# Forgetting attention with the values stationary and the weights of a group of query tiles moving

## The chip, the core and the metric

One core of a Trainium2 chip runs the whole program in one launch. The metric is the device time of an execution in microseconds. Five engines work side by side, each through its own list of instructions in order: PE (TensorE, matmuls; PEld is its weight load), VectorE (DVE), ScalarE (ACT), GpSimd (POOL) and SyncE (SP, which issues the DMAs). They wait for each other at semaphores. A matmul keeps one operand in the array (stationary, up to 128 x 128) and streams the other through it (moving); its result goes to one of eight PSUM banks of 128 x 512 fp32.

## What is computed

Two network blocks on 1024 tokens of width 1024. The part that the change touches is one of the three mixers of the second block: a causal attention of eight heads of 64 columns, on 1040 tokens (16 learned ones ahead of the 1024), in which each score gets the difference of two running sums of logarithmic forget gates.

```python
def forgetting_attention_group(q, k, v, f_logit, f_bias):
    ...
    qh = heads(q) * (HEAD_DIM ** -0.5)
    kh = heads(k)
    vh = heads(v)
    log_f = jax.nn.log_sigmoid((f_logit + f_bias).astype(jnp.float32))
    ...
    c = jnp.cumsum(log_f, axis=1).transpose(0, 2, 1)
    ...
        s = jnp.einsum('bhqd,bhkd->bhqk', qb, kh).astype(jnp.float32) + (cb[..., :, None] - c[..., None, :])
        s = jnp.where(kpos[None, :] <= qpos[:, None], s, -jnp.inf)
        p = jax.nn.softmax(s, axis=-1)
        return jnp.einsum('bhqk,bhkd->bhqd', p.astype(vh.dtype), vh)
```

Beside it stand a gated linear recurrence (RG-LRU) and RWKV7 with a state per head; the three results are joined and go through an output projection and a feed-forward network.

## The kernel before

**Numbers.** Most matmuls take operands of the type fp32r, and a value is kept as a rounded part (hi) and the remainder (lo): `split` casts hi on ScalarE (L103) and subtracts it from the source on VectorE (L106). A product is then two or three matmuls. The last product of this attention, weights times values, is an exception: it takes plain fp32, and the trace shows two passes on PE for each such matmul.

**Tiles.** The 1040 tokens are nine query tiles: one of 16 rows and eight of 128. A head is a pair index `pr` and a half `m` (64 of 128 columns). For each head the raw queries and keys come in by DMA (tag `fraw`), and ScalarE, VectorE and GpSimd make of them `fqh`, `fql`, `fkh`, `fkc` (L1471 to L1477), each in three buffers. The values `fv` of two heads come together.

**One query tile** (`fox_tile`, L1496 to L1534). The scores of tile i against all keys up to its own end are made in pieces of 400 and up to 512 columns: two matmuls (L1506, L1507), and on the last piece a third that adds the causal mask (L1509). VectorE moves each piece from PSUM to the tile `fE` and takes the row maximum in the same pass (L397); it reduces the maxima (L1514) and changes their sign (L1515, L1517). ScalarE takes the exponential in place and the row sum (L1519), VectorE the reciprocal (L1521). Then the weights have to be turned, since a matmul sums over partitions: `wT` transposes four key tiles at a time into a bank `te` (L405) and ScalarE copies it to `wT` (L407). L1531 multiplies: the turned weights are stationary, the 64 columns of the values move, and the sum over key tiles builds up in a bank `po`. VectorE scales the 64 result columns by the reciprocal (L1532). After the second head of a pair the rows go out (L1534).

**Order.** `fox_tile` has one `yield`, between the exponential and the transposes, and `pipe` runs the items so that the scores of a tile are recorded ahead of the second half of the tile before it. In which order each engine's list is written is decided by a scheduler of the framework, which models the time of the instructions as they are recorded. RWKV's chunks (`rwkv_chunks`) are recorded before this attention, and the scheduler mixes the two; at the end of the heads `done` loads the weights of the output projection (`woraw`, `wo`, L693 with L103 and L106), and the projection follows.

**Banks.** `psum` names for each use the groups of banks that it takes in turn: groups A, B and D have two banks each, C and E one. Before this attention the line `self.psum(sc="B", te="D", po="C")` gives scores two banks, transposes two, results one; RWKV uses A and E (`ra`, `rs`).

Of the kernel before, what the change touches and what calls it, by code (L numbers as in the profile page):

```python
# [13 lines left out]
F32 = mybir.dt.float32  # L14
F32R = mybir.dt.float32r
# [16 lines left out]
class Builder:  # L32
# [1409 lines left out]
    def fox_att(self, p, qkd, vd, cnd, o2d, done):  # L1442
# [7 lines left out]
        kcs = [p.tile([128, T], F32R, name=f"fkc{i}", bufs=1) for i in range(3)]  # L1450
# [5 lines left out]
        def heads():  # L1456
            for h in range(8):
# [9 lines left out]
                qh = p.tile([128, T], F32R, tag="fqh", name="fqh", bufs=3)  # L1467
                ql = p.tile([128, T], F32R, tag="fql", name="fql", bufs=3)
                kh = p.tile([128, T], F32R, tag="fkh", name="fkh", bufs=3)
                kc = kcs[h % 3]  # L1470
# [7 lines left out]
                if m == 0:  # L1478
                    v = p.tile([128, 9, 128], F32, tag="fv", name="fv")
# [3 lines left out]
                for i in range(9):  # L1483
                    yield self.fox_tile(pr, m, i, qh, ql, kh, kc, v, o, o2d)
# [4 lines left out]
    def fox_tile(self, pr, m, i, qh, ql, kh, kc, v, o, o2d):  # L1489

        nc, p = self.nc, self.ap_
        T = 1040
        r = slice(64 * m, 64 * m + 64)
        c0, n = self.TILES[i]
        nk = c0 + n
        if i == 0:  # L1496
            cks = [(0, 16)]
        else:
            cks = [(0, min(nk, 400))] + [(a, min(512, nk - a)) for a in range(400, nk, 512)]
        E = p.tile([128, T], F32, tag="fE", name="fE", bufs=4)  # L1500
        mx = self.small(4, "fmx")
        for ci, (k0, kn) in enumerate(cks):
            sp = self.sc()
            ks = slice(k0, k0 + kn)
            last = ci == len(cks) - 1
            nc.tensor.matmul(sp[:n, :kn], qh[:, c0:c0 + n], kh[:, ks], start=True, stop=False)  # L1506
            nc.tensor.matmul(sp[:n, :kn], ql[:, c0:c0 + n], kc[:, ks], start=False, stop=not last)  # L1507
            if last:
                nc.tensor.matmul(sp[:n, kn - n:kn], self.ident_r[:n, :n], self.masks_r[:n, 2, :n],  # L1509
                                 start=False, stop=True)  # L1510
            self.evac_max(E[:n, ks], sp[:n, :kn], mx[:n, ci:ci + 1])
        nM = self.small(1, "fnM")
        if len(cks) > 1:
            nc.vector.tensor_reduce(nM[:n], mx[:n, :len(cks)], axis=AX.X, op=ALU.max)  # L1514
            nc.vector.tensor_scalar(nM[:n], nM[:n], -1.0, None, op0=ALU.mult)  # L1515
        else:
            nc.vector.tensor_scalar(nM[:n], mx[:n, :1], -1.0, None, op0=ALU.mult)  # L1517
        l = self.small(1, "fl")
        nc.scalar.activation(E[:n, :nk], E[:n, :nk], AF.Exp, bias=nM[:n], accum_out=l[:n])  # L1519
        rl = self.small(1, "frl")  # L1520
        nc.vector.reciprocal(rl[:n], l[:n])  # L1521
        yield
        ops = self.po()
        steps = [(self.wT([E[:n, 0:16]], n), 0, 0)]
        for x0 in range(1, i + 1, 4):
            grp = range(x0, min(x0 + 4, i + 1))
            w = self.wT([E[:n, self.TILES[x][0]:self.TILES[x][0] + 128] for x in grp], n)
            steps += [(w, y, x) for y, x in enumerate(grp)]
        for w, y, x in steps:
            kn = self.TILES[x][1]  # L1530
            nc.tensor.matmul(ops[:n, :64], w[:kn, y, :n], v[:kn, x, r], start=x == 0, stop=x == i)  # L1531
        nc.vector.tensor_scalar(o[:n, i, r], ops[:n, :64], rl[:n], None, op0=ALU.mult)  # L1532
        if m == 1:
            nc.sync.dma_start(o2d[i][:, pr * 128:pr * 128 + 128], o[:n, i])  # L1534
# [413 lines left out]
```

## Time and profile before

| | us |
|---|---|
| median of three runs | 3181.07 (3169.08 to 3182.06) |
| profiled execution | 3179.39 |
| its span | 3177.6 |
| PE busy in the span | 3058.7 (96%) |
| VectorE | 1863.2 (59%) |
| ScalarE | 1401.9 (44%) |
| GpSimd | 467.1 (15%) |
| this attention, from the first score matmul to the projection | 283.1 |

The span is the time from the first to the last instruction in the profile; 1.8 us of the execution lie around it. Busy time counts an engine's instructions, not its waits. The granted clock (PEclk) is the share of full TensorE speed that the chip allowed in a stretch.

### The profile page before, as it was taken

What the parts mean: (1) busy time and instruction counts of PE and PEld (TensorE: products, weight loads), DVE (VectorE), ACT (ScalarE), POOL (GpSimd) and SP (SyncE); (2) the same over time, 40 slices, a digit from 0 to 9 for tenths busy, and PEclk for the clock granted to TensorE, in tenths of its full rate; (3) what the DMA queues carried; (4) which work ended last, traced back from release to release, by engine and by line L of the source; (5) the groups of instructions that cost most, each with busy time, mean ns of one, the idle gap of its engine ahead of it and who ended that gap; (6) DMA issues with size and microseconds to landing.
All of it is one profiled execution on the core that took longest, in us unless ns stands there. A gap on an engine that the chain in (4) does not pass through costs nothing.

```text
span 3177.6 us, 52057 instructions
## 1 busy us (share of the span) xinstructions
PE 3058.7 (96%) x19891; PEld 2780.7 (88%) x19891; DVE 1863.2 (59%) x4889; ACT 1401.9 (44%) x3415; POOL 467.1 (15%) x506
## 2 busy tenths in 40 slices
PE   8899999999999999998999999999999999999997
PEld 5799999889878789997889999788879999999996
DVE  5777757677766665446547434666555344454446
ACT  4679845555553643323236121445534433233323
POOL 2467622331220000000000000201000000000003
PEclk9999999999999999999999899898999999999999
DMA  5222210110043221113321121313132111111113
GB/s 212 71 74 89 85 40 6 32 33 7 15 138 107 100 101 57 57 39 101 126 67 49 58 69 46 90 41 97 34 123 94 49 40 47 47 47 57 44 41 116
DMA packets 140330, 218.22 MB, mean 69 GB/s; under 512 B 24408, under 2 KB 80784, under 8 KB 140080
## 3 DMA queue, kind: packets, MB, share of 16 engines
q1 hardware_dynamic: 140080, 214.90, 21.5%
q8 instruction: 156, 2.56, 0.3%
q14 instruction: 94, 0.77, 0.1%
HBM read 171.87 MB, written 42.97 MB: 68 GB/s over the span
## 4 chain that ended last, share of the span: by engine, by line
PE 80%; DVE 7%; ACT 5%; DMA 3%; issue 2%; POOL 1%; SPq 0%; DVEq 0%; POOLq 0%; ACTq 0%
PE mm L132 17%; PE mm L133 16%; PE mm L134 16%; PE po L1531 3%; PE te L405 3%; PE sc L134 2%; PE sc L132 2%; PE sc L133 2%; PE sc L391 2%; PE po L661 2%; PE po L611 1%; DMA woraw<-in_w_out 1%; ACT EB L646 1%; ACT EA L596 1%; PE mm L149 1%
## 5 line engine op out<-in xcount | busy, mean ns | idle before, releaser
L132 PE MATMUL mm<-whi,hT 128*128 128x256 f32 (+1 forms) x1760 | 513.4, 292 | 15.3 <-DVE gs L428 3.4
L133 PE MATMUL mm<-wlo,hT 128*128 128x256 f32 (+1 forms) x1760 | 508.3, 289 | 3.9 <-POOL wlo L106 3.8
L132 PEld LDWEIGHTS mm<-whi,hT 128*128 128x128 f32 x1760 | 337.6, 192 | 24.1 <-ACT v L549 4.6
L133 PEld LDWEIGHTS mm<-wlo,hT 128*128 128x128 f32 x1760 | 337.7, 192 | 8.0 <-POOL wlo L106 5.1
L132 PE MATMUL mm<-hT3h,whi 128*128 128x342 f32 (+3 forms) x1020 | 325.9, 320 | 0.0
L133 PE MATMUL mm<-hT3l,whi 128*128 128x342 f32 (+3 forms) x1020 | 325.2, 319 | 0.0
L134 PE MATMUL mm<-hT3h,wlo 128*128 128x342 f32 (+3 forms) x1020 | 324.7, 318 | 0.0
L134 PE MATMUL mm<-whi,lo 128*128 128x256 f32 x1040 | 300.0, 289 | 2.5 <-POOL lo L106 2.4
L103 ACT CAST whi<-wraw 128x512 fp32r<-128x512 f32 (+2 forms) x205 | 136.0, 678 | 211.2 <-PE mm L133 85.0
L132 PE MATMUL mm<-hT,whi 128*128 128x352 f32 (+3 forms) x640 | 219.8, 344 | 2.9 <-ACT a L1018 1.8
L1659 DVE TENSOR_TENSOR acc<-acc,sc 128x512 f32<-128x512 f32 x160 | 108.8, 686 | 193.6 <-PE sc L134 192.8
L407 ACT COPY wT<-te 128x512 f32<-128x512 f32 (+2 forms) x368 | 160.5, 454 | 136.3 <-PE te L405 133.5
L133 PE MATMUL mm<-hT,whi 128*128 128x352 f32 (+3 forms) x640 | 218.7, 342 | 0.1
L134 PE MATMUL mm<-hT,wlo 128*128 128x352 f32 (+3 forms) x640 | 218.5, 343 | 0.0
L106 DVE TENSOR_TENSOR wlo<-wraw,whi 128x512 fp32r<-128x512 f32 (+1 forms) x161 | 126.0, 790 | 152.2 <-ACT whi L103 151.5
L134 PE MATMUL mm<-whi,hT 128*128 128x256 f32 (+3 forms) x720 | 205.8, 286 | 0.0
L134 PEld LDWEIGHTS mm<-whi,lo 128*128 128x128 f32 x1040 | 201.0, 193 | 5.2 <-POOL lo L106 3.3
L133 PEld LDWEIGHTS mm<-hT3l,whi 128*128 128x128 f32 x1020 | 192.0, 188 | 6.3
L132 PEld LDWEIGHTS mm<-hT3h,whi 128*128 128x128 f32 x1020 | 191.8, 188 | 6.0
L134 PEld LDWEIGHTS mm<-hT3h,wlo 128*128 128x128 f32 x1020 | 191.9, 188 | 3.6
L97 POOL TENSOR_TENSOR inv<-inv,cm 128x1 f32<-128x1 f32 (+1 forms) x87 | 53.2, 611 | 889.1 <-DVE inv L95 889.1
L97 POOL TENSOR_TENSOR c<-c,cm 128x2 f32<-128x2 f32 (+1 forms) x170 | 124.4, 733 | 384.5 <-DVE c L95 346.0
(491 smaller groups left out, 7740.8 us busy)
## 6 DMA issues: line engine op xcount, KB each, us to landing
adraw<-in_adaln_w SPq DMA_DIRECT2D x48, 512.0 KB, 3.8
wraw<-in_ffn_up SPq DMA_DIRECT2D x85, 256.0 KB, 2.8
wraw<-in_w_ab SPq DMA_DIRECT2D x26, 512.0 KB, 3.9
woraw<-in_w_out SPq DMA_DIRECT2D x48, 256.0 KB, 3.0
wraw<-in_w_gla SPq DMA_DIRECT2D x48, 256.0 KB, 2.8
wraw<-in_w_in SPq DMA_DIRECT2D x24, 512.0 KB, 4.3
dnraw<-in_ffn_down SPq DMA_DIRECT2D x44, 256.0 KB, 2.6
fraw<-qkd SPq DMA_DIRECT2D x32, 260.0 KB, 4.1
```

The costliest lines, as they stand in the source:

```text
L97: nc.gpsimd.tensor_tensor(out, out, self.cm05[:p, :n], op=ALU.pow)
L103: nc.scalar.copy(hi, src)
L106: (lo_eng or nc.vector).tensor_tensor(lo, src, hi.bitcast(F32), op=ALU.subtract)
L132: mmul(ps, ah, bh, start=k == 0, stop=False)
L133: mmul(ps, ah, bl, start=False, stop=False)
L134: mmul(ps, al, bh, start=False, stop=k == nk - 1)
L391: self.nc.tensor.matmul(sp, q[x][:, m], keys, start=x == 0, stop=last and x == 1)
L405: nc.tensor.transpose(ps[:n, j * 128:j * 128 + nq], E, self.ident[:nq, :nq])
L407: nc.scalar.copy(w[:n, :m, :nq], ps.rearrange("p (j t) -> p j t", j=4)[:n, :m, :nq])
L661: nc.tensor.matmul(ops[:, :128], w[:, x, :], v[:, i], start=x0 + x == 0, stop=x0 + x == len(kt) - 1)
L1531: nc.tensor.matmul(ops[:n, :64], w[:kn, y, :n], v[:kn, x, r], start=x == 0, stop=x == i)
L1659: nc.vector.tensor_tensor(acc[:, t, sl], acc[:, t, sl], ps, op=ALU.add)
```

## The change

One item of work is now a group of query tiles instead of one: tiles 0 to 3, 4 to 6, 7 and 8. The values become the stationary operand: `fvs` holds for each key tile the 64 columns of hi and the 64 of lo side by side, 128 columns, made once per head by ScalarE and GpSimd. For each key tile the weights of all query tiles of the group that see it are transposed into one `te` bank, side by side, up to 400 columns. `split` makes hi (`feh`, ScalarE) and lo (`fel`, VectorE, from the bank), and both move through the values in two matmuls. The result in the `po` bank has the values' columns on the partitions, so at the group's end it is copied out (`fot`), transposed back, the two halves are added and scaled. The scores are stored with their sign changed, and the minimum takes the place of the maximum. Some buffers go from three or four to two, `fv` to one, and from head 5 on the transposes have four banks and the results two.

```diff
-        kcs = [p.tile([128, T], F32R, name=f"fkc{i}", bufs=1) for i in range(3)]
+        kcs = [p.tile([128, T], F32R, name=f"fkc{i}", bufs=1) for i in range(2)]
...
-                qh = p.tile([128, T], F32R, tag="fqh", name="fqh", bufs=3)
-                ql = p.tile([128, T], F32R, tag="fql", name="fql", bufs=3)
-                kh = p.tile([128, T], F32R, tag="fkh", name="fkh", bufs=3)
-                kc = kcs[h % 3]
+                qh = p.tile([128, T], F32R, tag="fqh", name="fqh")
+                ql = p.tile([128, T], F32R, tag="fql", name="fql")
+                kh = p.tile([128, T], F32R, tag="fkh", name="fkh")
+                kc = kcs[h % 2]
...
-                for i in range(9):
-                    yield self.fox_tile(pr, m, i, qh, ql, kh, kc, v, o, o2d)
+                vs = p.tile([128, 9, 2, 64], F32R, tag="fvs", name="fvs")
+                for z in ((slice(0, 128), slice(1, 9)), (slice(0, 16), slice(0, 1))):
+                    nc.scalar.copy(vs[z][:, :, 0], v[z][:, :, r])
+                    nc.gpsimd.tensor_tensor(vs[z][:, :, 1], v[z][:, :, r], vs[z][:, :, 0].bitcast(F32), op=ALU.subtract)
+                if h == 5:
+
+                    self.psum(te="DDA", po="CE")
+                for tiles in ((0, 1, 2, 3), (4, 5, 6), (7, 8)):
+                    yield self.fox_tiles(pr, m, tiles, qh, ql, kh, kc, vs, o, o2d)
...
-            self.evac_max(E[:n, ks], sp[:n, :kn], mx[:n, ci:ci + 1])
...
-            nc.vector.tensor_scalar(nM[:n], nM[:n], -1.0, None, op0=ALU.mult)
...
+                nc.vector.tensor_scalar(E[:n, ks], sp[:n, :kn], -1.0, None, op0=ALU.mult, op1=ALU.min,
+                                        accum_out=mx[:n, ci:ci + 1])
+            if len(cks) > 1:
+                nc.vector.tensor_reduce(nM[:n, y:y + 1], mx[:n, :len(cks)], axis=AX.X, op=ALU.min)
+            nc.scalar.activation(E[:n], E[:n], AF.Exp, bias=nM[:n, y:y + 1], scale=-1.0, accum_out=l[:n, y:y + 1])
...
-        steps = [(self.wT([E[:n, 0:16]], n), 0, 0)]
-        for x0 in range(1, i + 1, 4):
-            grp = range(x0, min(x0 + 4, i + 1))
-            w = self.wT([E[:n, self.TILES[x][0]:self.TILES[x][0] + 128] for x in grp], n)
-            steps += [(w, y, x) for y, x in enumerate(grp)]
-        for w, y, x in steps:
-            kn = self.TILES[x][1]
-            nc.tensor.matmul(ops[:n, :64], w[:kn, y, :n], v[:kn, x, r], start=x == 0, stop=x == i)
-        nc.vector.tensor_scalar(o[:n, i, r], ops[:n, :64], rl[:n], None, op0=ALU.mult)
+        for x in range(tiles[-1] + 1):
+            ys = [y for y, i in enumerate(tiles) if i >= x]
+            k0, kn = self.TILES[x]
+            ps = self.te()
+            for y in ys:
+                n = cols[y].stop - cols[y].start
+                nc.tensor.transpose(ps[:kn, cols[y]], Es[y][:n, k0:k0 + kn], self.ident[:n, :n])
+            z = slice(0, kn), slice(cols[ys[0]].start, c)
+            hi = p.tile([128, 400], F32R, tag="feh", name="feh", bufs=4)
+            lo = p.tile([128, 400], F32R, tag="fel", name="fel", bufs=4)
+            self.split(hi[z], lo[z], ps[z])
+            w = vs[:kn, x].rearrange("p e d -> p (e d)")
+            for e, h in enumerate((hi, lo)):
+                nc.tensor.matmul(ops[:, z[1]], w, h[z], start=x + e == 0, stop=e == 1 and x == tiles[-1],
+                                 skip_group_check=True)
+        ot = p.tile([128, 400], F32, tag="fot", name="fot")
+        nc.scalar.copy(ot[:, :c], ops[:, :c])
+        ps = self.te().rearrange("p (y e d) -> p y e d", y=4, e=2)
+        for y in range(len(tiles)):
+            n = cols[y].stop - cols[y].start
+            nc.tensor.transpose(ps[:n, y].rearrange("p e d -> p (e d)"), ot[:, cols[y]], self.ident)
+        t = p.tile([128, 4, 64], F32, tag="ft", name="ft")
+        parts = [(slice(0, 128), slice(small, len(tiles)))] + [(slice(0, 16), slice(0, 1))] * small
+        for rows, ys in parts:
+            nc.scalar.copy(t[rows, ys], ps[rows, ys, 1])
+            nc.vector.tensor_tensor(t[rows, ys], t[rows, ys], ps[rows, ys, 0], op=ALU.add)
+            shape = [rows.stop, ys.stop - ys.start, 64]
+            nc.vector.tensor_tensor(o[rows, tiles[0] + ys.start:tiles[0] + ys.stop, r], t[rows, ys],
+                                    rl[rows, ys].unsqueeze(2).to_broadcast(shape), op=ALU.mult)
```

In the changed program the score matmuls stand in L1519, L1520 and L1522, their evacuation in L1524, the exponential in L1528, the transposes in L1543, the two new matmuls in L1550, the copy out in L1553, the transposes back in L1557, the addition in L1562 and the scaling in L1564.

The order on PE in a head before, at the passage from one query tile to the next: `po` is the result's bank, `te` the transposes', `sc` the scores'; `x5` is five in a row.

```order
L1531 MATMUL po<-fv,wT 128x64 x4
L405 MATMUL te<-ident_r,fE 16x128
L1531 MATMUL po<-fv,wT 128x64 x2
L405 MATMUL te<-ident_r,fE 128x128 x7
L1531 MATMUL po<-fv,wT 128x64 x5
L405 MATMUL te<-ident_r,fE 16x128
L1506 MATMUL sc<-fkh,fqh 128x400
L1507 MATMUL sc<-fkc_23839,fql 128x400
L1531 MATMUL po<-fv,wT 128x64 x3
L405 MATMUL te<-ident_r,fE 128x128 x8
L1531 MATMUL po<-fv,wT 128x64 x5
```

In the changed program, in a head with two transpose banks, in the group of tiles 4 to 6 (three query tiles, 384 columns):

```order
L1543 MATMUL te<-ident_r,fE 16x128 x3
L1550 MATMUL po<-feh,fvs 128x384
L1550 MATMUL po<-fel,fvs 128x384
L1543 MATMUL te<-ident_r,fE 128x128 x6
L1550 MATMUL po<-feh,fvs 128x384
L1550 MATMUL po<-fel,fvs 128x384
L1543 MATMUL te<-ident_r,fE 128x128 x2
L1550 MATMUL po<-feh,fvs 128x384
L1543 MATMUL te<-ident_r,fE 128x128
L1550 MATMUL po<-fel,fvs 128x384
L1543 MATMUL te<-ident_r,fE 128x128 x3
```

Transposes and multiplications were taken by query tile, in runs of up to eight and five; now they alternate by key tile, three transposes and the two matmuls that read what the other engines made of the bank before.

On VectorE in a head before, score evacuations (L397) with one short scaling (L1532) and one reciprocal for each query tile:

```order
L1521 RECIPROCAL frl<-fl 128x1
L397 TENSOR_SCALAR fE,fmx<-sc 128x400
L1517 TENSOR_SCALAR fnM<-fmx 128x1
L397 TENSOR_SCALAR fE,fmx<-sc 128x400
L397 TENSOR_SCALAR fE,fmx<-sc 128x128
L1514 TENSOR_REDUCE fnM<-fmx 128x1
L1515 TENSOR_SCALAR fnM<-fnM 128x1
L1532 TENSOR_SCALAR fo<-po,frl 128x64
L1521 RECIPROCAL frl<-fl 128x1
L397 TENSOR_SCALAR fE,fmx<-sc 128x400
```

In the changed program the remainders (`fel` from the bank `te` and `feh`) stand between the score evacuations (L1524):

```order
L106 TENSOR_TENSOR fel<-te,feh 128x256
L1564 TENSOR_TENSOR fo<-ft,frl 128x3x64
L106 TENSOR_TENSOR fel<-te,feh 128x256 x6
L1524 TENSOR_SCALAR fE,fmx<-sc 128x400
L1524 TENSOR_SCALAR fE,fmx<-sc 128x128
L106 TENSOR_TENSOR fel<-te,feh 128x128
L1527 TENSOR_REDUCE fnM<-fmx 128x1
L1524 TENSOR_SCALAR fE,fmx<-sc 128x400
L106 TENSOR_TENSOR fel<-te,feh 16x400
L1524 TENSOR_SCALAR fE,fmx<-sc 128x256
L1524 TENSOR_SCALAR fE,fmx<-sc 128x400
L1527 TENSOR_REDUCE fnM<-fmx 128x1
```

The short scalings per query tile are gone, and L106 takes their place in larger number: each of these passes reads a whole bank's columns.

## Rows read from the trace of the kernel before

**Rows 1.** Windows of the attention: times, engines' busy us, granted clock, DMA share, GB/s

```profile
2022.60:2180.30 157.70, 157.42 (x1136) 137.39 (x1137) 113.29 (x413) 75.97 (x188) 22.36 (x23) 0.96 0.21 51
2180.30:2214.10 33.80, 31.93 (x172) 27.51 (x170) 20.02 (x73) 19.80 (x50) 2.79 (x2) 0.70 0.57 159
2214.10:2247.20 33.10, 30.27 (x193) 24.91 (x190) 21.91 (x78) 21.45 (x54) 2.96 (x2) 0.85 0.22 69
2247.20:2269.10 21.90, 21.86 (x166) 19.31 (x165) 11.70 (x58) 13.09 (x38) 0.00 (x0) 1.00 0.06 16
2269.10:2305.70 36.60, 36.17 (x278) 31.95 (x278) 14.81 (x73) 20.00 (x54) 0.00 (x0) 1.00 0.10 26
sum 283.10, PE 277.65 PEld 241.06 DVE 181.74 ACT 150.32 POOL 28.11; mean PE 55.53 PEld 48.21 DVE 36.35 ACT 30.06 POOL 5.62
```

**Rows 2.** Chain of waits from 2247 to 2270 us: start, duration, instructions

```profile
by line: PE po L1531 52.0%; PE te L405 21.5%; PE sc L1506 12.8%; PE sc L1507 10.2%; PE sc L1509 3.7%; issue 0.2%
...
2246.99 0.45 PE po L1531 x4
...
2256.61 0.88 PE te L405 x8
2257.49 1.40 PE po L1531 x10
...
2269.43 0.64 PE po L1531 x4
```

**Rows 3.** Timeline 484 to 487 us, in the first block: start, duration, instruction

```profile
484.01 0.38 PE L379 MATMUL tp<-ident_r,qn 128*128 128x128 f32 x2
...
484.62 0.37 ACT L103 CAST qTh<-tp 128x256 fp32r<-128x256 f32 x1
...
485.02 0.42 DVE L106 TENSOR_TENSOR qTl<-tp,qTh 128x256 fp32r<-128x256 f32 x1
...
485.22 0.28 PE L133 MATMUL mm<-wlo,hT 128*128 128x256 f32 x1
...
485.34 0.28 PE L134 MATMUL mm<-whi,lo 128*128 128x256 f32 x1
```

**Rows 4.** Timeline from 2208.9 us

```profile
2209.02 0.34 PE L1507 MATMUL sc<-fkc,fql 128*128 128x400 f32 x1
...
2209.20 0.40 PE L1506 MATMUL sc<-fkh,fqh 128*128 128x512 f32 x1
```

**Rows 5.** Groups of VectorE, shapes apart, 2022.6 to 2305.7 us: busy, mean ns | idle

```profile
L1532 DVE TENSOR_SCALAR fo<-po,frl 128x64 f32<-128x64 f32 x64 | 18.0, 281 | 38.3 <-PE po L1531 37.8
L1477 DVE TENSOR_TENSOR fkh<-fraw,fkh 64x1040 fp32r<-64x1040 f32 x7 | 10.6, 1509 | 1.8 <-ACT fkh L1475 1.6
...
L1521 DVE RECIPROCAL frl<-fl 128x1 f32<-128x1 f32 x64 | 10.2, 160 | 4.5 <-ACT fE L1519 1.9
...
L1472 DVE SCALAR_TENSOR_TENSOR fql<-fraw,fqh 64x1040 fp32r<-64x1040 f32 x7 | 9.1, 1301 | 1.6 <-DMA bd<-B 1.1 <-ACT fqh L1471 0.5
L1515 DVE TENSOR_SCALAR fnM<-fnM 128x1 f32<-128x1 f32 x40 | 5.8, 145 | 0.4
...
L1256 DVE TENSOR_TENSOR S<-STP,rs 64x128 f32<-64x128 f32 x8 | 2.3, 284 | 3.2 <-PE rs L1252 3.1
```

**Rows 6.** Groups of VectorE, shapes apart, whole span

```profile
L106 DVE TENSOR_TENSOR wo<-te,wo 128x512 fp32r<-128x512 f32 x26 | 17.8, 683 | 0.6 <-ACT wo L103 0.6
```

**Rows 7.** Groups of ScalarE, 2022.6 to 2305.7 us: together, then one shape

```profile
L407 ACT COPY wT<-te 16x128 f32<-16x128 f32 (+2 forms) x168 | 59.8, 375 | 73.9 <-PE te L405 71.6 <-PE sc L1509 1.1 <-PE po L1531 0.3
...
L407 ACT COPY wT<-te 128x384 f32<-128x384 f32 x16 | 7.6, 478 | 4.3 <-PE te L405 4.1
```

**Rows 8.** Groups of GpSimd, shapes apart, whole span

```profile
L106 POOL TENSOR_TENSOR wlo<-wraw,whi 128x512 fp32r<-128x512 f32 x44 | 62.0, 1430 | 39.1 <-ACT whi L103 39.0
```

**Rows 9.** Chain of waits from 2180 to 2195 us

```profile
2183.32 1.98 DVE fkh L1477
...
2185.68 2.58 PE po L1531 x10
```

More of the change, by code (lines that the diff above doesn't have):

```diff
@@ L1478, in heads @@
                 if m == 0:
-                    v = p.tile([128, 9, 128], F32, tag="fv", name="fv")
+                    v = p.tile([128, 9, 128], F32, tag="fv", name="fv", bufs=1)
                     nc.sync.dma_start(v[:16, 0], vd[0:16, pr * 128:pr * 128 + 128])
@@ L1485, in heads, with fox_tiles @@
+                if h == 5:
+                    self.psum(te="DDA", po="CE")
+                for tiles in ((0, 1, 2, 3), (4, 5, 6), (7, 8)):
+                    yield self.fox_tiles(pr, m, tiles, qh, ql, kh, kc, vs, o, o2d)
             done()
         self.pipe(heads())
-    def fox_tile(self, pr, m, i, qh, ql, kh, kc, v, o, o2d):
+    def fox_tiles(self, pr, m, tiles, qh, ql, kh, kc, vs, o, o2d):
         nc, p = self.nc, self.ap_
-        T = 1040
         r = slice(64 * m, 64 * m + 64)
[L1494 to L1510, printed above, removed]
-            self.evac_max(E[:n, ks], sp[:n, :kn], mx[:n, ci:ci + 1])
-        nM = self.small(1, "fnM")
-        if len(cks) > 1:
-            nc.vector.tensor_reduce(nM[:n], mx[:n, :len(cks)], axis=AX.X, op=ALU.max)
-            nc.vector.tensor_scalar(nM[:n], nM[:n], -1.0, None, op0=ALU.mult)
[L1516 to L1521, printed above, removed]
@@ new lines, in fox_tiles @@
+        ends = [c0 + n for c0, n in self.TILES]
+        E_ = p.tile([128, 1968], F32, tag="fE", name="fE")
+        l, nM = self.small(4, "fl"), self.small(4, "fnM")
+        Es, cols, a, c = [], [], 0, 0
+        for y, i in enumerate(tiles):
+            c0, n = self.TILES[i]
+            nk = ends[i]
+            E = E_[:, a:a + nk]
+            Es.append(E)
+            cols.append(slice(c, c + n))
+            a, c = a + nk, c + n
+            cks = [(0, min(nk, 400))] + [(x, min(512, nk - x)) for x in range(400, nk, 512)]
+            mx = nM[:, y:y + 1] if len(cks) == 1 else self.small(4, "fmx")
+            for ci, (k0, kn) in enumerate(cks):
+                sp = self.sc()
+                ks = slice(k0, k0 + kn)
+                last = ci == len(cks) - 1
+                nc.tensor.matmul(sp[:n, :kn], qh[:, c0:c0 + n], kh[:, ks], start=True, stop=False)
+                nc.tensor.matmul(sp[:n, :kn], ql[:, c0:c0 + n], kc[:, ks], start=False, stop=not last)
+                if last:
+                    nc.tensor.matmul(sp[:n, kn - n:kn], self.ident_r[:n, :n], self.masks_r[:n, 2, :n],
+                                     start=False, stop=True)
+                nc.vector.tensor_scalar(E[:n, ks], sp[:n, :kn], -1.0, None, op0=ALU.mult, op1=ALU.min,
[3 more added lines that the diff above has]
+            nc.scalar.activation(E[:n], E[:n], AF.Exp, bias=nM[:n, y:y + 1], scale=-1.0, accum_out=l[:n, y:y + 1])
@@ L1522, in fox_tile @@
+        rl = self.small(4, "frl")
+        small = 1 if tiles[0] == 0 else 0
+        if small:
+            nc.vector.reciprocal(rl[:16, :1], l[:16, :1])
+        nc.vector.reciprocal(rl[:, small:len(tiles)], l[:, small:len(tiles)])
         yield
         ops = self.po()
-        steps = [(self.wT([E[:n, 0:16]], n), 0, 0)]
-        for x0 in range(1, i + 1, 4):
-            grp = range(x0, min(x0 + 4, i + 1))
-            w = self.wT([E[:n, self.TILES[x][0]:self.TILES[x][0] + 128] for x in grp], n)
-            steps += [(w, y, x) for y, x in enumerate(grp)]
@@ L1533, in fox_tile @@
+        for rows, ys in parts:
[4 more added lines that the diff above has]
+                                    rl[rows, ys].unsqueeze(2).to_broadcast(shape), op=ALU.mult)
         if m == 1:
-            nc.sync.dma_start(o2d[i][:, pr * 128:pr * 128 + 128], o[:n, i])
+            for i in tiles:
+                n = self.TILES[i][1]
+                nc.sync.dma_start(o2d[i][:, pr * 128:pr * 128 + 128], o[:n, i])
```

## The prediction

> **What bounds the kernel now.** I read first the page's chain, which is mostly PE and names two lines of this attention, L1531 and L405, and then cut the attention out of the trace. It runs from the first score matmul of head 0 at 2022.6 us to about 2305.7 us. I cut that at the first score matmuls of heads 4, 5, 6 and 7, so that each stretch has one companion: heads 0 to 3 beside the RWKV chunks (157.7 us), heads 4 and 5 beside the loading of the output weights (33.8 + 33.1 = 66.9 us), heads 6 and 7 with the tail (21.9 + 36.6 = 58.5 us) [rows 1]. PE is busy for 277.65 of the 283.1 us. VectorE is busy for 181.74, ScalarE for 150.32, GpSimd for 28.11. The chain inside head 6 says the same in another way: it is PE from end to end, 52.0% of 23 us in L1531 (weights times values) and 21.5% in L405 (the transposes) [rows 2]. So PE sets this stage, and VectorE has about 100 us to spare in it. Only where heads 4 and 5 run is PE not full (31.93 of 33.8, 30.27 of 33.1), and there its granted clock is 0.70 and 0.85 of full.
>
> **What leaves PE.** A head has 45 pairs of query and key tile, and each L1531 matmul is two passes: 90 passes per head. The chain of head 6 holds fourteen pieces of L1531 with 88 passes in 52.0% of 23 us, 11.96 us: 0.136 us each [rows 2]. Removed: 90 x 0.136 = 12.2 us per head. The transposes stay, as many as before, at 0.88/8 = 0.11 us [rows 2].
>
> **What PE gets.** Per head 40 matmuls L1550 with the values stationary: 6 of 128 columns, 20 of 256, 14 of 384 or 400. The trace has this type at 256 columns in a row, 0.12 us from start to start [rows 3], and at 400 columns 0.18 [rows 4]. For 128 columns I take the transpose, 0.11. Sum 0.7 + 2.4 + 2.5 = 5.6. Nine transposes of the result (L1557) add 1.0. PE per head: -12.2 + 6.6 = -5.6 us, -45 us over eight heads. The Trainium skill ("TensorE: Matmul & The Clock Gate", "Back-to-back issue gap") has pairs of load and matmul at about 81 ns for 128 columns and 131 ns for 512. By it the forty would come to about 4.1 us, and all eight heads to 12 us less. The rows above are slower, and the sum goes by them.
>
> **What VectorE gets.** The remainders, 20 per head: 3 of 128 columns, 10 of 256, 6 of 384, 1 of 400, some on 16 rows only. A VectorE pass that reads PSUM takes 0.284 at 128 columns [rows 5], 0.418 at 256 [rows 3], 0.683 at 512 [rows 6]; 384 and 400 lie between, 0.55 and 0.57. Sum 0.85 + 4.2 + 3.3 + 0.6 = 8.9 us. The four additions L1562 and four multiplications L1564 per head, 64 to 192 columns, are not in the trace. At least 0.28 each (the 64-column L1532), at most 0.418 (256 columns): 2.2 to 3.3, I take 2.5. Removed: nine L1532 at 0.281 (2.5), nine negations at 0.145 (1.3), five of nine reciprocals at 0.16 (0.8) [rows 5]. The evacuation of the scores is one pass with a minimum in place of a maximum: no change. VectorE per head: +6.8 us, +54 us in all.
>
> **What the others get.** ScalarE: 168 copies L407 of 59.8 us go; 160 casts come, 80 of 256 columns at 0.37 [rows 3], 48 of 384 at 0.478 [rows 7], the rest less or about as much, 64 us, and the copies of the result and of the values some 3 us per head. It stays near 180 of 283 us: cover enough. GpSimd gets one remainder of the values of 512 elements per head, about 1.43 [rows 8], beside 28 us of work: hidden, except at a head's start, where the first L1550 would wait for it.
>
> **Buffers.** Two in place of three for the prepared queries and keys. The preparation's two VectorE passes (1.301 + 1.509 = 2.8 us [rows 5]) can then be done at most one head ahead, so one preparation moves into the last stretch: +2.8 us of VectorE there. Its cover is the head before, 20 us of other work; without the cover it costs a stop like that at the start of head 4, where PE waited through 1.98 us of L1477 and went on at half clock, ten passes in 2.58 us against 1.40 [rows 9, 2]. I take nothing, and keep 0 to 5 us per head in the range. From head 5 on there are four banks for transposes and two for results. RWKV's last matmul stands before that head in either order, so taking its banks costs nothing.
>
> **The sum.** Neither engine can go below its own work, and the stage was never shorter than PE's. Stretch by stretch [rows 1]:
> - Heads 0 to 3: PE 157.4 - 22.4 = 135.0; VectorE 113.3 + 27.2 = 140.5. Floor 140.5, before 157.7.
> - Heads 4 and 5: PE 62.2 - 11.2 = 51.0 and the 4.7 us that it stood still, 55.7; VectorE 41.9 + 13.6 = 55.5. Floor 55.7, before 66.9.
> - Heads 6 and 7: PE 58.0 - 11.2 = 46.8; VectorE 26.5 + 13.6 + 2.8 = 42.9. Floor 46.8, before 58.5.
>
> The floors add up to 243. The stage before stood 2% above its floor, but with one full engine beside idle ones. Now two are equally full and hand work to each other twice for each key tile, so I take the middle between floor and before in each stretch, a choice and not a row: 149.1 + 61.3 + 52.7 = 263, 20 us less. The profiled execution took 3179.39 us, its span 3177.6 and 1.8 around it, 1.7 under the median shown. 3179.4 - 20 = 3160 us, nearly (0.6%). What is late next is VectorE in the first two stretches.
>
> **The handover in detail.** A key tile of 256 columns holds its bank while PE transposes (0.38 for two), ScalarE casts (0.37) and VectorE subtracts (0.42, started 0.40 after the cast) [rows 3]: about 1.25 us with the handovers, 0.62 per tile with two banks. PE's own work for it is 2 x 0.11 + 2 x 0.12 = 0.46. Twenty such tiles make 12.5 us per head, under a head's 21.9 before, so the loop alone doesn't set the time. It does where VectorE is not ready, since score evacuations and RWKV passes stand between the subtractions. In the order shown above VectorE has six subtractions in a row and then nine rows with two among them. A late remainder holds up the L1550 that reads it and all that PE has behind it: the transposes of the next key tiles and the next scores, for which VectorE then waits in its turn.
>
> **Rivals.**
> *PE's gain comes through* (chance 0.22). The other work fills PE's waits and VectorE runs near its floor. The floors give -40; 5 to 10 above them, -33: 3146 us. For it: RWKV and the scores of the next group are independent work. Against it: VectorE would have to be over 94% busy (235 of 250 us), and it was at 64% in this stage [rows 1].
>
> *Slower: the two-bank loop paces PE and lowers its clock* (0.23). Place: heads 0 to 4, which have two banks for transposes. With VectorE late, PE idles at every key tile. In this trace the granted clock is 0.70 and 0.85 just where PE waited in the stage [rows 1], and ten passes took 2.58 us instead of 1.40, 1.84 times as long [rows 9, 2]. PE's work for a head alone is 21.9 - 5.6 = 16.3 at the full level (2.4 GHz), 30.0 at the half level (1.2 GHz): 8 us more than before. Five heads wholly at the half level: +41; half of that time, +20: 3200 us. It decides once PE is at the half level for over about 40% of these heads, since (1.84 - 1) x 16.3 x 0.41 eats the 5.6. Against it: heads 0 to 3 have RWKV matmuls in every gap (granted 0.96). The Trainium skill ("TensorE: Matmul & The Clock Gate", "A second HAM failure mode: psum-queue depth-cycling") reports a kernel that cycled through PSUM banks, idled briefly between groups of matmuls, and lost throughput to an oscillating clock. By that rule this rival would be the case; the trace agrees in so far as the clock fell in heads 4 and 5, but not in head 6, where the same cycle through two banks ran at 1.00.
>
> *Nothing to measure* (0.08). What PE gains it waits for VectorE: +54 on VectorE against -45 on PE, and the stage stays at 283 within 5 us: 3179.
>
> **How the numbers follow.** The forecast, VectorE becomes an equal bound and eats about half of the gain, has 0.47; its own range is 3150 to 3176. A measurement of this kernel tells about 0.5%, 16 us, from no change: faster is below 3165, slower above 3197. Of the forecast's chance about 0.28 lies below 3165 and 0.19 above. Faster: 0.28 + 0.22 = 0.50. Slower: 0.19 of the slower rival. Within: 0.19 + 0.08 + 0.04 = 0.31. The range is 3140 to 3203: the floors at its low end, and at the high end the slower rival to a little above its middle; what it leaves out, longer stretches at the half clock and PE passes cheaper than the rows, is under 2 in 10.
>
> **What would show it.** PE busy in the stage near 233 us and VectorE near 235, the stage near 263. L1550 spaced 0.12 us at 256 columns; L106 on the bank 0.42. Among the waits, PE at L1543 or L1550 waiting for VectorE's L106 should take the place that L1531 had in the chain. A granted clock of 0.9 or more in heads 0 to 3 and 6 to 7. It is wrong if the PE clock falls in heads 0 to 4 (slower), if L106 takes far from 0.42, or if the stage shrinks by over 30 us (VectorE then had more room than I gave it).

## The result: slower by half a per cent

The changed kernel takes 3198.0 us (median of seven runs, 3194.45 to 3203.33) against 3181.07 before (3169.08 to 3187.66). The ratio is 1.0057, 95% interval 1.0042 to 1.0071: 17 us slower, where 21 us faster was forecast. The profiled execution took 3203.33 us, the slowest of the seven, span 3201.6.

Up to the attention the two traces differ by 5 us (before issues its first load at 2000.8 us, after at 2005.5), at the first score matmul by 3.5, and behind the attention the distance stays at 23 to 24 us to the end. So some 20 us of the difference were made in the attention. Its windows in the changed kernel, cut at the first score matmuls of heads 3 and 5 and at the last scaling (columns as in [rows 1]):

```profile
2026.10:2153.30 127.20, 123.24 (x840) 103.76 (x839) 103.47 (x344) 60.88 (x153) 21.48 (x23) 0.97 0.21 51
2153.30:2231.10 77.80, 63.10 (x267) 44.32 (x268) 52.92 (x158) 46.69 (x118) 7.83 (x9) 0.76 0.39 108
2231.10:2329.00 97.90, 86.79 (x493) 67.20 (x493) 69.12 (x235) 61.47 (x170) 7.37 (x8) 0.91 0.10 26
sum 302.90, PE 273.13 PEld 215.28 DVE 225.50 ACT 169.04 POOL 36.67; mean PE 91.04 PEld 71.76 DVE 75.17 ACT 56.35 POOL 12.22
```

The stage is 302.9 us long, before it was 283 [rows 1]. No engine fills it: PE is busy for 273, VectorE for 225.5. The first window holds three heads and all of RWKV, which ended at 2139 us (before at 2170); PE is nearly full there and its clock is 0.97. An estimate: if a head without RWKV took 21.9 us before, as head 6 did [rows 1], RWKV took 157.7 - 4 x 21.9 = 70, and the three heads of this window took 19 each. By that the change gained beside RWKV. The five heads after it took 175.7 us, 35 each, with a granted clock of 0.76 and 0.91; before, four such heads took 125.4, 31 each.

What PE waits for in these five heads (total us, times, longest), from its own and its weight loads' rows:

```profile
PEld po L1550 <- ACT feh L103: 22.4, 30, 3.3
PEld po L1550 <- DVE fel L106: 17.4, 38, 2.5
PE po L1550 <- ACT feh L103: 13.8, 13, 3.0
PE po L1550 <- DVE fel L106: 5.8, 8, 2.2
```

In the four comparable heads before, the longest sum of this kind was 4.4 us. A round is what one key tile goes through: transposes into a bank, the cast, the subtraction, the two matmuls. A piece of the timeline shows how the wait is made, in head 4 with two banks, at full clock:

```profile
2217.21 0.39 PE L1550 MATMUL po<-fel,fvs 128*128 128x256 f32 x1
2217.43 0.38 PE L1543 MATMUL te<-ident_r,fE 128*128 128x128 f32 x2
2217.45 0.78 ACT L103 CAST feh<-te 128x256 fp32r<-128x256 f32 x2 [0.75 <-PE te L1543]
2217.85 0.83 DVE L106 TENSOR_TENSOR fel<-te,feh 128x256 fp32r<-128x256 f32 x2 [0.70 <-ACT feh L103]
2217.87 0.38 PE L1550 MATMUL po<-feh,fvs 128*128 128x256 f32 x1
2218.33 0.39 PE L1550 MATMUL po<-fel,fvs 128*128 128x256 f32 x1
2218.55 0.28 PE L1550 MATMUL po<-feh,fvs 128*128 128x256 f32 x1
2218.67 0.38 PE L1543 MATMUL te<-ident_r,fE 128*128 128x128 f32 x2
...
2219.01 0.38 PE L1543 MATMUL te<-ident_r,fE 128*128 128x128 f32 x2
2219.09 0.37 ACT L103 CAST feh<-te 128x256 fp32r<-128x256 f32 x1 [0.86 <-PE te L1543]
```

The cast starts at 2217.45 and again at 2219.09: 1.64 us for two key tiles, 0.82 each. Between the casts ScalarE stood idle for 0.86 us ahead of the second start, VectorE waited for the cast, and PE waited twice: for `feh`, and at 2218.33 for `fel`, with the next transposes behind it in its list. The engines work one after the other, and none of them is full.

The single durations came out as they were priced. VectorE's groups in the stage (busy us, mean ns):

```profile
L106 DVE TENSOR_TENSOR fel<-te,feh 128x256 fp32r<-128x256 f32 x72 | 29.0, 422 | 16.8 <-ACT feh L103 16.4
...
L106 DVE TENSOR_TENSOR fel<-te,feh 128x384 fp32r<-128x384 f32 x40 | 21.5, 551 | 11.3 <-ACT feh L103 11.1
...
L1562 DVE TENSOR_TENSOR ft<-ft,te 128x192 f32<-128x192 f32 x16 | 5.6, 348 | 2.3 <-ACT ft L1561 2.2
L1564 DVE TENSOR_TENSOR fo<-ft,frl 128x192 f32<-128x192 f32 x16 | 5.4, 340 | 0.0
```

And L1550 in a row at full clock, where RWKV keeps PE busy: 2067.77 - 2067.59 = 0.18 us at 384 columns.

```profile
2067.59 0.34 PE L1550 MATMUL po<-fel,fvs 128*128 128x384 f32 x1
...
2067.77 0.34 PE L1550 MATMUL po<-feh,fvs 128*128 128x384 f32 x1
```

### The profile page after: what moved, and what is told of

Read it like the earlier page. It is cut to its first block, busy times and chain, and to the rows that moved or that the text cites. A ratio compares the mean times of both kernels' runs of the same rounds, so it can differ in the third digit from the quotient of the medians.

```text
span 3201.6 us, 51514 instructions
## 1 busy us (share of the span) xinstructions
PE 3062.0 (96%) x19563; PEld 2764.0 (86%) x19563; DVE 1909.4 (60%) x4929; ACT 1420.6 (44%) x3478; POOL 479.5 (15%) x522
## 4 chain that ended last, share of the span: by engine, by line
PE 78%; DVE 9%; ACT 6%; DMA 4%; issue 2%; POOL 1%; SPq 0%; DVEq 0%; POOLq 0%; ACTq 0%
PE mm L132 17%; PE mm L133 16%; PE mm L134 16%; PE sc L134 2%; PE sc L133 2%; PE sc L132 2%; PE sc L391 2%; PE po L661 2%; PE te L405 2%; PE po L1550 1%; PE po L611 1%; DMA woraw<-in_w_out 1%; ACT EB L646 1%; PE te L1543 1%; ACT EA L596 1%
## 5 line engine op out<-in xcount | busy, mean ns | idle before, releaser
L106 DVE TENSOR_TENSOR wlo<-wraw,whi 128x512 fp32r<-128x512 f32 (+1 forms) x161 | 125.9, 790 | 151.7 <-ACT whi L103 150.9
L1674 ACT COPY fx<-mm 128x342 f32<-128x342 f32 (+2 forms) x132 | 58.7, 445 | 253.8 <-PE mm L134 253.0
```

What stands on the lines that cost most here:

```text
L106: (lo_eng or nc.vector).tensor_tensor(lo, src, hi.bitcast(F32), op=ALU.subtract)
L1674: nc.scalar.copy(x[:, c0 - 14:c0 - 14 + n], ps[:, :n])
```

## The experiments

All are edits of the changed kernel, except where before is named. Ratios are against the kernel before, run on the same chip, with 95% intervals; "stage" is the attention in the one profiled execution, from the first score matmul to the last scaling. Stages of single executions are good to a few us: two runs with nearly equal medians (e1, e14) have stages 7 us apart. The framework's scheduler writes the engines' lists anew for each version, so a run shows its edit together with the order that came of it.

### What the remainder costs

**e1**, no subtraction:

```diff
-            self.split(hi[z], lo[z], ps[z])
+            nc.scalar.copy(hi[z], ps[z])
...
-            for e, h in enumerate((hi, lo)):
+            for e, h in enumerate((hi, hi)):
```

> The changed kernel without VectorE's subtraction on the transposes' bank; both L1550 matmuls of a key tile read feh, so PE does the same work (the remainder is left out of the result). Theory 1, the handover: PE waits in the round transposes -> cast -> subtraction -> matmul -> next transposes, about 1.64 us for two key tiles of 256 columns in heads 3 and 4, and its clock falls in those waits. Without the subtraction the round is about 0.44 us shorter: some 4 us per head in the five heads after RWKV, and the clock back in part: 3165 to 3180 us, granted clock there over 0.90. Theory 2, VectorE's throughput: 8.9 us per head off the bounding engine, the stage falls to PE's floor near 235 us: 3135 to 3150. Theory 3, only the earlier end of RWKV and the output weights' loading beside fewer matmuls: no change, 3195 to 3200.

Measured: 3162.3 us, ratio 0.9943 (0.9927 to 0.9959), 36 us less than the changed kernel; stage 274.7. That is a little more than the handover was said to cost and 12 us short of what VectorE's throughput would have given; it did not decide.

**e2**, the subtraction reads a tile in SBUF (as many columns, other numbers), so the bank is free after the cast:

```diff
-            self.split(hi[z], lo[z], ps[z])
+            nc.scalar.copy(hi[z], ps[z])
+            nc.vector.tensor_tensor(lo[z], E_[:kn, 16 + z[1].start:16 + z[1].stop], hi[z].bitcast(F32), op=ALU.subtract)
```

> The changed kernel with the subtraction reading a tile in SBUF (the exponentials, not turned) in place of the bank: as many VectorE passes of the same sizes, the second L1550 still waits for them, but a bank is free after the cast (the remainder is a wrong one). Theory 1: the next transposes can start 0.4 us earlier, but the second matmul still stands ahead of them in PE's list: a part of the gain of the run without subtraction, 3180 to 3192 us. Theory 2 (VectorE's throughput): nothing, 3195 to 3200.

Measured: 3175.36, ratio 0.9986 (0.9973 to 1.0000); stage 281.3. With all of VectorE's passes in place 23 us are gone. Throughput predicted nothing and falls; the gain is also larger than the handover theory said.

**e3** leaves the line with the freed banks out; **e4** has it at head 3 (`if h == 3:`).

> The changed kernel with two banks for the transposes and one for the results in all heads. Theory 1: in head 6 a round of three key tiles took 1.65 us with four banks, 0.55 each, in head 4 1.64 for two, 0.82 each: 20 x 0.27 = 5 us per head in heads 5 to 7, and more waits at the half clock: 3210 to 3225 us. Theory 2: no change, 3195 to 3200.

> The changed kernel with the freed banks from head 3 on (RWKV's last matmul was at 2139 us, head 3 began at 2153) in place of head 5. Theory 1: about 5 us each in heads 3 and 4, 3183 to 3193 us. Theory 2 or 3: no change, 3195 to 3200.

Measured: e3 3218.0, ratio 1.0118 (1.0083 to 1.0153), stage 323.4; e4 3186.67, ratio 1.0011 (0.9995 to 1.0028), stage 288.3. Both in the range of the handover: banks are time here, some 20 us for heads 5 to 7 and 11 for heads 3 and 4. The kernel before hardly cares (**e8**, the freed banks from head 5 on in it):

> The kernel before with the freed banks alone from head 5 on (transposes four, results two). Its transposes fill a bank with four key tiles and PE waited there for under 10 us in heads 4 to 7: 3175 to 3181, hardly to be told from no change.

Measured: 3177.33 against 3177.82, ratio 1.0009 (0.9989 to 1.0030): no change.

**e13 and e14** take three things apart: the hold (the bank stays taken until the subtraction has read it), the wait (PE's second matmul needs the remainder) and VectorE's work itself. e13 is the changed kernel with `enumerate((hi, hi))` alone; e14 is e2 with it.

> The changed kernel with the subtraction reading the bank as before, while the second L1550 reads feh and so doesn't wait for it (the remainder is left out of the result). The stage was 302.9 us in the changed kernel and 274.7 without the subtraction. Theory H, the bank's hold costs: the stage stays near 296, 3191 us. Theory W, the wait of the second matmul at the head of PE's list costs: near 280, 3168 to 3175.

> The changed kernel with the subtraction reading SBUF and the second L1550 reading feh: VectorE's work is there, but no bank is held for it and PE doesn't wait for it (the remainder is left out). The run with an early free bank and the wait had 281.3 us. If VectorE's time itself costs: near 281, 3175 us. If only hold and wait cost: near 275, 3162 to 3166.

Together with e1 and e2 (median us; stage in brackets):

| | PE's second matmul waits for the subtraction | it doesn't wait |
|---|---|---|
| bank held through the subtraction | 3198.0 (302.9), the change | 3174.8 (279.9), e13 |
| bank free after the cast | 3175.4 (281.3), e2 | 3160.7 (267.4), e14 |
| no subtraction at all | | 3162.3 (274.7), e1 |

e13's ratio is 0.9997 (0.9987 to 1.0006), e14's 0.9948 (0.9933 to 0.9963). By these medians the wait is worth 23 us while the bank is held, the hold 23 us while PE waits, both together 37; by the ratios, each against the kernel before on its own chip, 19, 23 and 35. VectorE's 70 us of subtractions by themselves are worth nothing that can be measured: e14 has them and e1 has not, at the same time (145.0 and 145.5 us from head 3 on). The order on PE is not the same in the four versions: from head 3 on its list passes from transposes to L1550 93 times in the changed kernel, 65 times in e13, 58 in e2 and 68 in e14. How much of each step is this order was not measured by itself. The windows from head 3 to the end, of e13, e2 and e14:

```profile
2141.80:2298.50 156.70, 133.55 (x752) 104.93 (x753) 121.21 (x394) 105.81 (x284) 17.72 (x16) 0.87 0.25 71
```
```profile
2154.90:2308.70 153.80, 134.65 (x752) 106.00 (x753) 122.06 (x398) 105.64 (x284) 18.38 (x17) 0.89 0.26 72
```
```profile
2142.10:2287.10 145.00, 125.26 (x750) 98.89 (x749) 120.87 (x393) 104.14 (x283) 20.67 (x17) 0.93 0.27 77
```

VectorE is busy for 121 or 122 us in all three, as in the changed kernel (52.92 + 69.12 = 122.0); the stretch shrinks from 175.7 to 156.7, 153.8 and 145.0, and the granted clock rises from 0.84 over the stretch (0.76 and 0.91 above) to 0.93 without anything having been done to it. PE's busy time falls with it, from 63.10 + 86.79 = 149.9 to 125.3 us for the same work, so a part of the 31 us between the changed kernel and e14 may be the clock's.

### The clock

**e10**, e3 with three more transposes per key tile from head 3 on:

```diff
             for e, h in enumerate((hi, lo)):
+                if e and self.warm:
+                    for j in range(3):
+                        nc.tensor.transpose(self.spare[:, j * 128:j * 128 + 128], self.ident, self.ident)
```

> The run with two banks in all heads (3218 us), with three more transposes of the identity per key tile from head 3 on, into an otherwise unused bank, ahead of the second L1550, where PE waits for VectorE: 0.33 us of more PE work at full clock, 33 us in five heads. Theory 1a, the clock is a large part of the loss: PE stays at the full level, the dummies lie in the waits, and the time is the same or falls to 3200 to 3218 with a granted clock over 0.95 in heads 3 to 7. Theory 1b, the clock is only a by-product and the waits themselves are the loss: the dummies cost a part of their 33 us, 3220 to 3245.

Measured: 3243.79, ratio 1.0194 (1.0169 to 1.0219), in the range for the clock as a by-product, but for a reason that wasn't foreseen: the scheduler put 201 of the 327 dummies ahead of head 3 (27 belong to head 2's last group), where PE is full, and the window up to head 3 grew from 127.1 to 145.8 us. The other 126 lie in the first 23 us of head 3, which began at 2169.5; heads 4 to 7 have none:

```profile
L1552 PE MATMUL spare<-ident_r x327: 270/273/328, 2133.9 to 2192.9; 128*128 128x128 f32 x164
```

Heads 3 and 4 in e3, then in e10:

```profile
2150.10:2229.40 79.30, 63.98 (x279) 44.56 (x279) 53.95 (x158) 46.81 (x119) 8.18 (x9) 0.78 0.37 104
```
```profile
2169.50:2247.70 78.20, 68.07 (x405) 51.68 (x403) 48.85 (x149) 41.88 (x108) 8.15 (x9) 0.96 0.26 70
```

The clock went from 0.78 to 0.96, PE got some 14 us of work more (126 x 0.11), and the two heads took the same time. That doesn't decide: the dummies may have taken back what the clock gave, and e10 has less other work there (VectorE 149 passes in place of 158).

Two other comparisons of these traces show what the clock costs. Heads 5 to 7 have no dummies in e10 and run the same program as in e3, at a lower clock. e3, then e10:

```profile
2229.40:2346.40 117.00, 99.02 (x481) 69.20 (x482) 70.95 (x234) 63.40 (x169) 7.47 (x8) 0.90 0.09 23
```
```profile
2247.70:2368.50 120.80, 105.81 (x480) 75.03 (x481) 71.44 (x234) 63.70 (x169) 7.49 (x8) 0.81 0.08 21
```

With two levels, a granted clock of 0.90 is 2 x 0.10 x 117.0 = 23 us at the half level, and 0.81 is 46 us; 22.5 us more at the half level cost 3.8 us. The other comparison is of four key tiles of 256 columns of head 4, from cast to cast, with two banks in both. The changed kernel, then e3:

```profile
2216.32:2219.43 3.11, 2.87 (x16) 1.94 (x15) 1.41 (x4) 1.46 (x4) 0.00 (x0) 1.00 0.22 63
```
```profile
2213.82:2217.93 4.11, 4.03 (x17) 3.18 (x16) 1.47 (x5) 1.49 (x4) 0.00 (x0) 0.58 0.17 47
```

Where the round paces PE, a clock of 0.58 makes it a third longer: 1.00 us for 2 x 0.42 x 4.11 = 3.5 us at the half level. In the five heads the changed kernel is at the half level for about 55 us (2 x 0.24 x 77.8 + 2 x 0.09 x 97.9), e14 for about 20 (2 x 0.07 x 145.0). An estimate from these two rates, 0.17 and 0.29 us per us: the clock makes up 6 to 10 of the 31 us between them, and the waits without it the larger part.

### The buffers

**e11**, the kernel before with two buffers in place of three for the prepared queries and keys (`range(2)`, `kcs[h % 2]`, no `bufs=3`):

> The kernel before with two instead of three buffers for the prepared queries and keys alone. If the preparation stays hidden behind the head before: no change, 3175 to 3183. If PE waits for it at each head's start as at head 4 (some 2 us and a half clock after it): 2 to 5 us per head, 3190 to 3210.

Measured: 3186.34 against 3181.62, ratio 1.0017 (1.0003 to 1.0031): some 5 us slower (1 to 10), between the two cases. Its trace has the loss in one place, head 5, which took 46 us (2211.0 to 2257.0) where it was 33; head 4 took 30 where it was 34.

### Versions that might beat both

**e5** is e4 with as many key tiles in a bank as fit 512 columns, 14 rounds per head in place of 20; **e6** is e4 without the split, one fp32 matmul per key tile with the 64 value columns stationary (`fv` has two buffers again there); **e7** is both. All three, and the runs that are made from e5, also take the groups of banks in the order D, A, where e4 takes D, D, A: a bank of group D comes round after four key tiles or packs in place of three. The edits of e5 and of e6, cut:

```diff
+        for xs, width in packs:
+            ps = self.te()
...
+            z = slice(0, kn), slice(0, at)
+            hi = p.tile([128, 512], F32R, tag="feh", name="feh", bufs=4)
+            lo = p.tile([128, 512], F32R, tag="fel", name="fel", bufs=4)
+            self.split(hi[z], lo[z], ps[z])
+            for x, src, dst in offs:
```
```diff
-            self.split(hi[z], lo[z], ps[z])
+            nc.scalar.copy(w[z], ps[z])
...
+            nc.tensor.matmul(ops[:64, z[1]], v[:kn, x, r], w[z], start=x == 0, stop=x == tiles[-1],
+                             skip_group_check=True)
```

> The run with the freed banks from head 3, and as many key tiles in a bank as fit into 512 columns: 14 rounds per head in place of 20, each with one cast and one subtraction. PE does the same work, VectorE's remainders go from 8.9 to about 8.0 us per head. Theory 1 (the handover round): a quarter of the rounds goes; with about 0.55 us of round per key tile of 256 columns some 3 us per head, 3165 to 3178 us. Theory 2 (VectorE's throughput): 1 us per head, 3178 to 3182. If a longer round in each bank eats it: 3187.

> The run with the freed banks from head 3, without the split: ScalarE copies the turned weights in fp32, one fp32 matmul with the 64 value columns stationary takes the place of the two (it shows as two passes, which before took the weights' time at 64 columns; at 256 columns an fp32 pass is not in the trace of this attention, PE per head +1 to +5 us), and no addition of halves at the end. No VectorE pass stands between bank and matmul. Theory 1: the round loses the subtraction as in the run without it, 3165 to 3178 us with PE's longer passes. Theory 2: VectorE has 11 us less per head, same. Against both: if fp32 passes of 256 columns cost over 0.3 us each, PE is the bound again and the time is 3185 or more.

> As the fp32 run, with up to 512 columns of key tiles in a bank: 14 in place of 20 rounds. If the round still paces PE there, 3 us per head less than the fp32 run; if PE's passes bound it, the same.

Measured: e5 3176.68, 0.9991 (0.9981 to 1.0000), stage 278.7. e6 3188.75, 1.0037 (1.0023 to 1.0051): PE is the bound again, busy for 292.6 of 296.6 us of the stage. e7 3179.62, 1.0005 (0.9995 to 1.0015); PE is busy for 94.45 of 97.4 us from head 5 on. So packing together with the other order of banks gains 10 us by the medians (6 by the ratios); the order was not tried alone. fp32 gives up on PE what it saves on VectorE.

**e9**, e5 with the bank copied out first, hi made by VectorE and the remainder by GpSimd from SBUF (three buffers each in place of four):

```diff
-            self.split(hi[z], lo[z], ps[z])
+            nc.scalar.copy(wt[z], ps[z])
+            nc.vector.tensor_copy(hi[z], wt[z])
+            nc.gpsimd.tensor_tensor(lo[z], wt[z], hi[z].bitcast(F32), op=ALU.subtract)
```

> The run with packed banks, with ScalarE copying a bank to SBUF in fp32 (the bank is free after that), VectorE casting hi from there and GpSimd subtracting (1.43 us for 512 columns, some 15 us per head beside a head of about 25 us). Theory 1, the bank's hold is what paces: the hold falls by a third and the result stays exact, 3160 to 3172 us. If instead the whole length of the round to the second matmul paces (it grows by about 1 us), or GpSimd becomes the bound: 3180 to 3200.

Measured: 3209.01, ratio 1.0085 (1.0065 to 1.0105), stage 310.3: 32 us slower than e5. The bank no longer waits for a subtraction, but GpSimd takes 1.37 us for 512 columns and 1.11 for 384, and the second matmul has to wait for that. GpSimd itself is busy for 168 of 310 us. So a longer round to the second matmul costs, which fits the wait's column of the table.

**e12**, e5 without the subtraction, both matmuls reading `feh`:

> The run with packed banks without the subtraction, the second matmul reading feh (the remainder is left out). Theory 1: what the subtraction still costs when there are fewer rounds and four banks; it was 36 us with 20 rounds and banks freed at head 5. If the bank's hold was nearly all of it, 8 to 15 us are left: 3162 to 3169. If VectorE's throughput were behind it, 25 to 36 as before: 3141 to 3152.

Measured: 3143.6, ratio 0.9883 (0.9857 to 0.9909); 33 us below e5, where 8 to 15 were expected. That is in the range that was written down for VectorE's throughput (3141 to 3152). e12 takes out hold, wait and VectorE's work together, so in the packed form none of the three is excluded; what e1 and e14 show of VectorE's work holds for the changed kernel with its 20 rounds. Its stage:

```profile
sum 247.40, PE 233.64 PEld 200.82 DVE 165.38 ACT 160.14 POOL 38.84; mean PE 77.88 PEld 66.94 DVE 55.12 ACT 53.38 POOL 12.95
```

**e15, e16, e17, e18** record the second matmul one bank later (e15 on e5; e16, on e5 too, two banks later; e17 on the changed kernel; e18 on e4). The edit of e17 and e18, cut:

```diff
+            late.append((1, x, w, lo, z))
+            for e, x_, w, h, z in [(0, x, w, hi, z)] + ([late.pop(0)] if len(late) > 1 else []) + \
+                    (late if x == tiles[-1] else []):
```

> The run with packed banks, with the second matmuls of a bank recorded behind the first ones of the next bank. Theory W: PE has the next round's work ahead of the wait, some 10 to 20 us less than 3177: 3157 to 3167. Theory H or VectorE's time: no change, 3173 to 3180.

> The same with the second matmuls two banks behind. Theory W: at least as good as one bank behind, 3150 to 3167, unless fel's four buffers now hold up the subtractions. Theory H or VectorE's time: no change, 3173 to 3180.

> The changed kernel with the second L1550 of a key tile recorded behind the first one of the next; nothing else. If the wait can be moved in this way, the stage falls from 302.9 towards the 279.9 us of the run without the wait: 3176 to 3188. If the next key tile's first matmul can't come earlier because its bank is held until the subtraction is done (two banks), nothing is gained: 3195 to 3200.

> The same with the freed banks from head 3 on (3187 us without it): with four banks the next key tile's work is there when PE comes to it. If the wait is what is left: 3170 to 3180, below the packed run's 3177 if both work. If not: 3185 to 3189.

Measured: e15 3173.33, 0.9989 (0.9979 to 0.9999); e16 3180.11, 1.0010 (1.0000 to 1.0019); e17 3196.49, 1.0056 (1.0037 to 1.0074); e18 3184.05, 1.0009 (0.9997 to 1.0022). The remedy fails: e15, e17 and e18 stand within 0.0002 of the ratios of e5, the change and e4, and e16 is 0.2% above e5. e17's waits after RWKV:

```profile
PEld po L1553 <- ACT feh L103: 27.0, 39, 2.4
...
PEld te L1544 <- DVE fel L106: 5.7, 9, 1.2
```

The wait for `fel` at the second matmul is gone but for 1.9 of 17.4 us, but the first matmul now waits 27.0 in place of 22.4, and the transposes wait for the bank. An explanation that fits: with both banks in use, work that could stand ahead of the wait needs a bank which the same subtraction still holds. It isn't shown, and with more banks (e18) the wait for `fel` also moved, from 12.6 to 1.6 us against e4, and the first matmul's grew from 17.1 to 22.2. e15 is the fastest exact version, 0.1% below the kernel before (0 to 0.2%): that is no gain worth its code.

## Why the prediction was wrong

- **PE's work, -45 us**: right as work, but PE's busy time in the changed kernel was 273.1 us and not 233. A lone L1550 of 256 columns shows 0.38 us where [rows 3] has 0.12 from start to start, and at the half level it takes longer still (0.56 to 0.58 in e3). e12, which gives PE the change's matmuls and waits least, has PE busy for 233.6 us.
- **VectorE's work, +54 us**: measured +43.8 (225.5 - 181.7); the single durations 0.422, 0.551 and about 2.4 us for L1562 and L1564 per head are as priced. The durations of all its passes add up to 51 us more than before (213.9 to 265.3); the rest is overlap between neighbouring instructions.
- **"I take the middle between floor and before"**: this is the step that failed. It takes the two engines' shares as what limits the stage, and lets the handover cost no more than the half way back to the time before, 20 us above the floors of 243. The stage came out 60 us above them. What was missing is hold and wait, 35 to 37 us with the lower clock that goes with them. With both taken out and all of the work left in (e14), the stage is 267.4 us and the kernel 3160.7, where 263 and 3160 were forecast. That this agrees is luck as far as the reason goes: the forecast rested on VectorE as an equal bound, and e1, with 70 us less of VectorE's work, takes the same time.
- **"The loop alone doesn't set the time"**: the same error, in the working. The bank's hold was put at 1.25 us; the row itself has 1.43, from the first transpose at 484.01 to the subtraction's end at 485.44 [rows 3]. Dividing it by two banks, 0.62 per key tile, needs the two banks to be filled and emptied in alternation. In PE's list the next transposes stand behind the matmul that waits for the remainder, so fill, cast, subtraction and multiplication follow each other, and it is 0.82 at full clock. Twenty rounds of 0.82 make 16.4 us, still under the 21.9 of a head before, so the rounds alone don't make a head of 35 us: what else PE has in a head must come largely on top of them and not in their waits. How much each part adds was not measured. Where RWKV's matmuls stand in between, heads 0 to 2, little of it shows (127.2 us, and 122.4 in e14); heads 3 to 7 have no such cover.
- **The buffers, "I take nothing"**: about 5 us in the kernel before (e11); in the change it wasn't measured by itself.
- **The slower rival** (3200 us) has the number by luck and much of the mechanism. Its +20 us don't follow from its own figures: with 16.3 us at the full level and 30.0 at the half level, half of the work at the half level makes five heads 6 us longer, and +20 needs 70% of it. The two-bank loop does pace PE and the clock does fall, which the prediction had named as the sign of this rival; but not in heads 0 to 2 (0.97), rather where RWKV is gone, in heads 3 and 4 (0.76) and less in 5 to 7 (0.91). And the clock is the smaller part of the loss by the estimate above, and came back by itself where the waits went. The Trainium skill ("TensorE: Matmul & The Clock Gate", "A second HAM failure mode: psum-queue depth-cycling") was cited for it. The trace agrees with what it says of brief idle between groups and of a lower clock; in this kernel the waits themselves are the larger loss.
- **Nothing to measure** and **PE's gain comes through**: both fall; the latter's 3146 is near what e12 gives (3143.6), which leaves the remainder out.

Open: what holds e14 at 145.0 us from head 3 on, where PE is busy for 125.3 and VectorE for 120.9; and where the last 33 us between e5 and e12 sit, since in e5 PE waits for VectorE at two places (11.5 us in transposes for the addition that ends a group, 11.0 for the remainder), and neither was taken out alone there.

## What to carry to other kernels

Two engines that hand work to each other within one round don't add up by busy time: count the round, from the bank's first write to the next write that may follow it, in the order of each engine's list, and divide by the banks only if that list really lets them alternate. In this kernel a step added between a bank and the matmul that reads it cost twice, by holding the bank and by making PE wait, and taking away either gave back 19 to 23 of some 35 us; only moving the matmul later gave back nothing (e15 to e18). A lower clock came with the waits and made the rounds longer in its turn, so it is no separate cause, but part of the price. And look at what covers such a round: here it cost little as long as another mixer's matmuls lay in between.

## What the runs showed of the hardware

GpSimd's subtraction of 512 fp32 columns took 1.37 us where VectorE's takes 0.68, and VectorE's took the same from SBUF or from PSUM at that size (0.686 for `woraw`, 0.683 for `te` in [rows 6]). The same rounds on the same two banks took 3.11 us at a granted clock of 1.00 and 4.11 at 0.58, while 22.5 us more at the half level, spread over three heads, cost 3.8 us (e3 and e10). GpSimd's groups in e9 (busy us, mean ns):

```profile
L1565 POOL TENSOR_TENSOR fel<-few,feh 128x384 fp32r<-128x384 f32 x64 | 70.1, 1106 | 49.0 <-DVE feh L1564 41.4 <-PE po L1569 4.8 <-PE sc L1522 1.3
L1565 POOL TENSOR_TENSOR fel<-few,feh 128x512 fp32r<-128x512 f32 x24 | 32.6, 1370 | 21.4 <-DVE feh L1564 20.3 <-DVE rwvar L95 1.1
```
